# Layer 0's opening: tile 0's rows and two modulation blocks load first, and four gate tiles run as two halves over the input features

## The chip, the cores and the metric

The kernel runs on one core of a Trainium2 chip. The metric is the device time of one execution in microseconds (us). The core has five engines that work beside each other: TensorE (PE, matrix products, with its weight loads shown apart as PEld), VectorE (DVE), ScalarE (ACT), GpSimd (POOL) and SyncE (SP, which here issues most DMA transfers). Each engine takes its instructions in a fixed order. "Granted clock" is the share of full speed that TensorE ran at.

## The reference, cut to what matters

A backbone of two layers: layer 0 is windowed attention with a gate, layer 1 a bidirectional scan mixer. The change touches only the start of layer 0:

```python
shift, scale, gate = adaln(c, w_ada[i], b_ada[i])         # silu(c) @ w_ada + b_ada, split in 3
shift_c, scale_c, gate_c = adaln(c_ctx, w_ada[i], b_ada[i])
u  = rms_normalize(h)  * (1.0 + scale[:, None]) + shift[:, None]
uc = rms_normalize(hc) * (1.0 + scale_c) + shift_c
...
q, k, v, g = jnp.split(h @ w_in, [...], axis=-1)          # h is u or uc here
...
y_lat = ((o * jax.nn.silu(g)) @ w_out)
```

There are 1024 latent rows, 256 context rows and 1024 features, all in float32.

## The kernel before, in words

Everything is held transposed: features on the 128 partitions (8 tiles `k` of 128 features), rows along the free axis. The rows form three tiles `i`: tile 0 and tile 1 with 512 latent rows each, tile 2 with the 256 context rows. A float32 matrix product is done as three products of rounded halves: `mm3` (L225 to L231) multiplies the high half of the weights `wh` with the high and the low half of the rows (`uH`, `uL`), and the low half `wl` with `uH`. `load_w` loads a weight tile into a `wr` buffer (7 of them); ACT rounds it to `wh` (L215) and POOL subtracts to get `wl` (L217), four buffers each. `load_halves` does a weight tile as two halves over the input features.

The opening is `norm0`. It needs shift and scale: four blocks `n` of the modulation weights (0 and 1 are shift, 2 and 3 scale; 0 and 2 serve features k = 0 to 3, 1 and 3 serve k = 4 to 7). `ada0` multiplies one block with the condition on TensorE (L372), copies the row on ACT and turns it into a column (`modulation`). The blocks use eight `wada` buffers, four for each block. For each tile of rows, `stats` squares on ACT, adds the eight squares (L416, on POOL), and `rstd_c` sums over partitions on TensorE (L354), takes root and reciprocal and spreads the factor r with another product (L361, copied by ACT in L363). `modulate` then makes `uH` and `uL` of each k. It has two forms: without POOL, DVE multiplies by scale and r (L296), ACT adds the shift and rounds (L297), DVE adds and subtracts (L298); with POOL, POOL multiplies by r (L291), DVE scales and shifts (L292), ACT rounds (L293), DVE subtracts (L294). `N0P` says for how many k of each tile the form with POOL is used.

After it, `qkvg` runs on tile 0 the four gate tiles (`g_step`, `g_out`), then for each tile the two k tiles (`kproj`, with the rotation `rope` on DVE and POOL) and the v blocks of 128 rows (`vproj`, weights `wv`, copied from `pj` by ACT in L541 and DVE in L542). `pj` has four banks. `v` and the k tensors lie in a pool that takes the memory of norm0's pool, so they can be written only once what lay there has been used. Later come the q tiles, other gates and the modulation columns of the rest, and attention.

The order on each engine is made when the program is built: a scheduler takes, among the instructions that are ready by its own estimate of time, the one with the lowest place in the program. `high_priority(offset=-U0OFF[i])` shifts the places of a block: `U0OFF` of 100 puts it 100 places later, -200 puts it 200 places earlier. `issue_after(ins)` keeps the transfers that a block issues behind `ins` on its queue. The order of the loads is modulation block 0, tile 0's rows, blocks 2, 1 and 3 (`XORD`), the weights of the first two gates, tile 1's rows, the rope tables, tile 2's rows, the other weights.

Of the kernel before, what the change touches and what calls it, by code (L numbers as in the profile page):

```python
# [9 lines left out]
F32 = mybir.dt.float32  # L10
# [3 lines left out]
ALU = mybir.AluOpType  # L14
# [3 lines left out]
P = 128  # L18
D = 1024
KT = D // P  # L20
LAT = 1024
# [4 lines left out]
TT = [(0, 512), (512, 512), (1024, 256)]  # L26

HEADS = 16
KV = 4
HD = 64  # L30
# [12 lines left out]
    pj=1, S=2, pt=2, pv=1,  # L43
# [1 line left out]
    oraw=3, h1=2, h1k=8, wada=8, sqa=1,  # L45
    cacc=2, cctx=1, bT=2, cT=2, xn4=4, xn2=1, bn4=4, bn2=1, sz=2, xw=2, hf=2, hx=2, M=2, y2=1, xs=1, uT=2, pj2=2, psX=3, sk=2, dg=2,
)
N0P = (0, 4, 4)
ADAO = 0
XORD = (0, "x", 2, 1, 3)  # L50
VLAST = 0
G0 = 4
U0OFF = (0, 100, 200)
AHEAD = 1
PACE = 4
PARTS = 8
# [51 lines left out]
class Kernel:  # L108
# [196 lines left out]
    def layer0(self):  # L305
        nc, t, a = self.nc, self.t, self.a
        cps = ExitStack()
        BUFS.update(S=1, pj=4, wr=7, qf=2, ql=2, wh=4, wl=4)
        self.psA = self.pool("psA", space=PSUM, ctx=cps)
        NB = (LAT + CTX) // P  # L310
        self.uH, self.uL = [None] * 3, [None] * 3
        cw = ExitStack()
        wvp = self.pool("wv", ctx=cw)

        self.cs = t(wvp, [P, KT, 32], F32, "cs32")
        nc.vector.memset(self.cs, 0.0)
        nc.vector.tensor_copy(self.cs[:, :, 0:2], self.csf)
        self.wp = self.pool("wq", ctx=cw)
        p = self.pq = self.pool("qp", ctx=cw)
        c0 = ExitStack()  # L320
        n0 = self.norm0(c0)
        next(n0)
        wg = [self.load_halves(a["wg"][x], nc.gpsimd) for x in range(2)]
        next(n0)
        self.load_rope(p, 0, LAT)
        next(n0)
        c0.close()
        ckv = ExitStack()
        kvp = self.pool("kv", ctx=ckv, side="right")
        self.v = t(kvp, [P, NB, KV, 2 * HD], F32R, "v")  # L330
        self.kHH = [t(kvp, [P, LAT + CTX], F32R, f"kHH{j}") for j in range(KV)]
        self.kL = [t(kvp, [P, LAT + CTX], F32R, f"kL{x}") for x in range(KV // 2)]
        self.mask = t(kvp, [P, 1152], BF16, "mask")
        self.nsink = t(kvp, [P, HEADS], F32, "nsink")
        self.sink = t(kvp, [P, HEADS], F32, "sink")
        self.qkvg(p, wg, wvp)
        if "u" in self.dump:
            for i, (s, n) in enumerate(TT):
                self.dump_split("u", self.uH[i], self.uL[i], i, n, s)
        cw.close()  # L340
        cps.close()
        with ExitStack() as c1:
            BUFS.update(S=2, pj=1)
            self.psA = self.pool("psT", space=PSUM, ctx=c1)
            self.attention(c1, ckv)
            BUFS.update(pj=2)

    def rstd_c(self, pool, acc, n, width, size=512, rout=None, dout=None):

        nc, t, ps = self.nc, self.t, self.psA  # L350
        nb = n // P
        pn = t(ps, [P, 512], F32, self.ptag)
        for b in range(nb):
            nc.tensor.matmul(pn[:, b : b + 1], acc[:, b * P : (b + 1) * P], self.ones[:, 0:1], start=True, stop=True)  # L354
# [6 lines left out]
        nc.tensor.matmul(pr[:, :n], self.ones, dg.rearrange("p b n -> p (b n)"), start=True, stop=True)  # L361
        r = t(*(rout or (pool, [P, size], F32, f"rr{size}")))[:, :n]
        nc.scalar.copy(r, pr[:, :n])  # L363
        return r
# [9 lines left out]
        nc.scalar.copy(row, pj)  # L374
        self.modulation(0, n, row, ps)

    def norm0(self, c0):

        nc, t = self.nc, self.t
        ps = self.psA  # L380
        p1 = self.p0 = self.pool("n0", ctx=c0, side="right")

        u = self.up
        hin, hs = {}, {}
        raws = {}

        def load_x(i):
            src = self.xin(i).rearrange("(k p) n -> p k n", p=P)
            if i == 0:
                x = t(u, [P, KT, 512], F32, "uL1")  # L390
                hin[i] = [x[:, :4], x[:, 4:]]
            elif i == 1:
                hin[i] = [t(u, [P, KT // 2, 512], F32, tag) for tag in ("uH2", "uL2")]
            else:
                hin[i] = [t(p1, [P, 2, 512], F32, "wada").rearrange("p k n -> p (k n)").rearrange("p (k n) -> p k n", k=4) for _ in range(2)]
            hs[i] = [x[:, k] for x in hin[i] for k in range(4)]
            for e in range(2):
                ld = nc.sync.dma_start(hin[i][e], src[:, 4 * e : 4 * e + 4])
            return ld

        def load_ada(n):
            raws[n] = [t(p1, [P, 2, 512], F32, "wada") for e in range(4)]
            for e in range(4):
                ld = nc.sync.dma_start(raws[n][e], self.a["w_ada"][0, n, 2 * e : 2 * e + 2].rearrange("k p c -> p k c"))
            return ld

        def stats(i):
            n = TT[i][1]
            acc = t(p1, [P, 512], F32, "sqa")[:, :n]
            for k in range(KT):  # L410
                if k == 0:
                    nc.scalar.activation(acc, hs[i][k], AF.Square)
                else:
                    sq = t(p1, [P, 512], F32, "sqt")[:, :n]
                    nc.scalar.activation(sq, hs[i][k], AF.Square)
                    nc.gpsimd.tensor_tensor(acc, acc, sq, op=ALU.add)  # L416
            return self.rstd_c(p1, acc, n, D)

        for n in XORD:
            if n == "x":  # L420
                load_x(0)
            else:
                ld = load_ada(n)
        with self.tc.issue_after(ld.ins):
            yield
            ld = load_x(1)
        with self.tc.issue_after(ld.ins):
            yield
            load_x(2)
        r = stats(0)  # L430
        if ADAO:
            for n in (0, 2, 1, 3):
                self.ada0(n, raws[n], ps)
            for k in range(8):
                self.alloc_u(0) if k == 0 else None
                self.modulate(0, hs[0][k], r, 0, k, N0P[0] > k)
        else:
            for e in range(2):
                for n in (e, 2 + e):
                    self.ada0(n, raws[n], ps)  # L440
                if e == 0:
                    self.alloc_u(0)
                for k in range(4 * e, 4 * e + 4):
                    self.modulate(0, hs[0][k], r, 0, k, N0P[0] > k)
# [6 lines left out]
        yield  # L451

    def rope(self, pool, ps, i, out):
        nc = self.nc
# [49 lines left out]
    def g_step(self, p, w, x, i):  # L504
        self.g_out(p, self.proj_h(self.psA, w, self.uH, self.uL, i), x, i)

    def qkvg(self, p, wg, wvp):
# [8 lines left out]
        self.q_d = [[t(self.dr, [4, 2, HD, n], F32, f"q{j}_{i}") for i, (_, n) in enumerate(TT)] for j in range(KV)]  # L516
        self.sg_d = [[t(self.dr, [2, P, n], F32, f"sg{j}_{i}") for i, (_, n) in enumerate(TT)] for j in range(KV)]


        for x in range(G0):  # L520
            self.g_step(p, wg[x] if x < 2 else self.load_halves(a["wg"][x], nc.gpsimd), x, 0)
        wk = [self.load_halves(a["wk"][x], nc.gpsimd) for x in range(2)]
        wv = [self.load_w(a["wv"][q // 2, :, q % 2 * 512 : q % 2 * 512 + 512], 2, 256, pool=wvp, eng=nc.gpsimd) for q in range(4)]

        def kproj(x, i):
# [35 lines left out]
        n = [3, 3, 3, 2]  # L561
# [983 lines left out]
```

## Time and profile before

| | |
|---|---|
| time, median of 3 runs | 1880.89 us (1879.43 to 1883.35) |
| the profiled execution's own time | 1880.79 us, span 1878.7 us |
| mean granted clock of TensorE | 0.98 |
| busy shares of the span | PE 95%, DVE 63%, ACT 48%, POOL 40% |
| the opening, 0 to 104 us | first gate matmul at 35.19, first k matmul of tile 1 at 104.16 |

A row of the timeline gives the start, the length, the engine, the line, the operation, the output and input by the program's names, the shape and the count, and in brackets how long the engine had stood idle and what ended that. A row with a count above one spans from the first start to the last end. A row of a group gives busy time and mean length of one in ns; a row of waits gives who waited for whom, the sum, the number of times and the longest.

### The profile page before, as it was taken

How to read it: one execution, taken by the hardware profiler on the slowest of the kernel's cores; microseconds unless marked ns; L12 is line 12 of the kernel's file. 1: busy time of each engine (PE TensorE's matmuls, PEld its weight loads, DVE VectorE, ACT ScalarE, POOL GpSimd, SP SyncE). 2: the span in 40 equal slices, each digit the busy share in tenths (PEclk: the TensorE clock that was granted, in tenths of full speed). 3: DMA queues.
4: the chain of work that ended last, by engine and by line, in shares of the span. 5: the costliest groups of instructions: out<-in, count | busy, mean ns of one | idle time of the engine just before them, and what ended most of it. 6: DMA issues, size and time to landing. Idle time of an engine off the chain costs nothing. (4 is left out here: it accounts for less than half of the span.)

```text
span 1878.7 us, 29635 instructions
## 1 busy us (share of the span) xinstructions
PE 1790.6 (95%) x10632; PEld 1541.9 (82%) x10632; DVE 1178.2 (63%) x2199; ACT 906.5 (48%) x1861; POOL 758.8 (40%) x1029
## 2 busy tenths in 40 slices
PE   6899998899999899979999999999999999999997
PEld 2687776788888786668898898989889898988887
DVE  3754426887777766584665758666575766754843
ACT  4522326677778665562353535434353544543632
POOL 4741107654456454302343343524335252442411
PEclk8899999999999999989999999999999999999998
DMA  9348756553345446111111111111111111433552
GB/s 357 108 118 260 240 167 157 126 126 95 97 120 134 113 129 222 59 56 34 38 36 44 47 33 44 39 41 36 44 47 33 47 38 39 141 117 100 177 153 78
DMA packets 147203, 192.10 MB, mean 102 GB/s; under 512 B 15312, under 2 KB 84816, under 8 KB 147056
## 3 DMA queue, kind: packets, MB, share of 16 engines
q1 hardware_dynamic: 112992, 171.56, 29.0%
q0 software_dynamic: 34064, 18.65, 5.5%
q8 instruction: 84, 1.38, 0.3%
q14 instruction: 63, 0.52, 0.1%
HBM read 154.54 MB, written 35.92 MB: 101 GB/s over the span
## 5 line engine op out<-in xcount | busy, mean ns | idle before, releaser
L229 PE MATMUL pj<-uH,wh 128*128 128x512 f32 (+1 forms) x712 | 259.3, 365 | 12.1 <-DVE v L542 2.8
L230 PE MATMUL pj<-uL,wh 128*128 128x512 f32 (+1 forms) x712 | 245.1, 345 | 1.3 <-DVE uL L298 0.9
L231 PE MATMUL pj<-uH,wl 128*128 128x512 f32 (+1 forms) x712 | 244.5, 344 | 1.1 <-POOL wl L217 1.1
L1059 POOL TENSOR_TENSOR xw<-xn,dtdec 128x256 f32<-128x256 f32 x144 | 105.9, 738 | 206.6 <-PE psD L1082 102.1
L984 PE MATMUL pj<-uH,wh 128*128 128x512 f32 x512 | 171.7, 405 | 1.1 <-ACT xn L951 1.1
L984 PE MATMUL pj<-uH,wl 128*128 128x512 f32 x512 | 171.8, 405 | 0.0
L229 PEld LDWEIGHTS pj<-uH,wh 128*128 128x128 f32 x712 | 136.7, 192 | 40.5 <-issue 11.9
L984 PE MATMUL pj<-uL,wh 128*128 128x512 f32 x512 | 168.3, 399 | 0.0
L217 POOL TENSOR_TENSOR wl<-wr,wh 128x512 fp32r<-128x512 f32 x96 | 127.2, 1329 | 77.7 <-ACT wh L215 67.1
L631 DVE TENSOR_TENSOR pl<-pt,ph 128x512 fp32r<-128x512 f32 x168 | 114.5, 687 | 64.6 <-ACT ph L630 63.5
L1009 PE MATMUL pj<-wh,uH 128*128 128x256 f32 x512 | 154.7, 302 | 0.0
L1009 PE MATMUL pj<-wh,uL 128*128 128x256 f32 x512 | 151.3, 295 | 0.0
L231 PEld LDWEIGHTS pj<-uH,wl 128*128 128x128 f32 x712 | 136.4, 192 | 17.7 <-POOL wl L217 1.5
L1009 PE MATMUL pj<-wl,uH 128*128 128x256 f32 x512 | 150.8, 295 | 0.0
L230 PEld LDWEIGHTS pj<-uL,wh 128*128 128x128 f32 x712 | 136.9, 192 | 14.0 <-DVE uL L298 1.4
L215 ACT CAST wh<-wr 128x512 fp32r<-128x512 f32 (+1 forms) x136 | 87.3, 643 | 116.8 <-PE pj L230 75.2
L1188 ACT ACTIVATE uT<-psX,nw 128x128 f32<-128x128 f32 x128 | 47.0, 367 | 189.9 <-PE psX L1187 188.8
L605 DVE CUSTOM_DVE_ANT_0 sm<-S,mask,nsink 128x640 f32<-128x640 f32 (+2 forms) x160 | 119.1, 772 | 26.7 <-PE S L602 13.8
L630 ACT CAST ph<-pt 128x512 fp32r<-128x512 f32 x168 | 97.6, 586 | 61.8 <-PE pt L626 56.2
L607 ACT ACTIVATE sm<-sm,nm 128x640 f32<-128x640 f32 (+2 forms) x160 | 118.5, 742 | 9.5 <-DVE nm L605 9.0
L1154 POOL TENSOR_TENSOR xs<-xn,sk 128x256 f32<-128x256 f32 x64 | 42.0, 657 | 184.8 <-DVE sk L1150 183.6
L984 PEld LDWEIGHTS pj<-uL,wh 128*128 128x128 f32 x512 | 95.6, 188 | 19.9
(330 smaller groups left out, 4990.5 us busy)
## 6 DMA issues: line engine op xcount, KB each, us to landing
wr<-w_x SPq DMA_DIRECT2D x32, 512.0 KB
wr<-wo SPq DMA_DIRECT2D x48, 256.0 KB
wr<-w_sk SPq DMA_DIRECT2D x24, 512.0 KB
wr<-wg SPq DMA_DIRECT2D x40, 256.0 KB
qs<-q POOLq DMA_DIRECT2D x40, 256.0 KB, 4.0
wada<-w_ada SPq DMA_DIRECT2D x16, 512.0 KB
wr<-wq SPq DMA_DIRECT2D x32, 256.0 KB
wl<-w_ada SPq DMA_DIRECT2D x32, 256.0 KB
```

The costliest lines, as they stand in the source:

```text
L215: nc.scalar.copy(h, raw)
L217: (eng or nc.vector).tensor_tensor(l, raw, h, op=ALU.subtract)
L229: self.nc.tensor.matmul(ps, lh, rh, start=first and i == 0, stop=False)
L230: self.nc.tensor.matmul(ps, lh, rl, start=False, stop=False)
L231: self.nc.tensor.matmul(ps, ll, rh, start=False, stop=last and i == n - 1)
L605: nc.vector.tensor_tensor_reduce(out=sm[:, :W], in0=Sv, in1=self.mask[:, m0 : m0 + W], scale=-SCALE, scalar=self.nsink[:, 4 * j + r : 4 * ...
L607: nc.scalar.activation(sm[:, :W], sm[:, :W], AF.Exp, bias=nm[:, r : r + 1], scale=-1.0, accum_out=sums[:, r : r + 1])
L630: nc.scalar.copy(ph, ptf)
L631: nc.vector.tensor_sub(pl, ptf, ph)
L984: nc.tensor.matmul(raw[:, 512 * i : 512 * i + 512], l[:, k, :], r[i][:, k, :], start=k + y == 0, stop=k == KT - 1 and y == 2)
L1009: nc.tensor.matmul(pj[:, c], l, r[:, k, :], start=c % 2 + q + k + y == 0, stop=c % 2 == 1 and q == 1 and k == 3 and y == 2)
L1059: nc.gpsimd.tensor_tensor(xw, X(st, c).rearrange("p (r h) -> p r h", r=R), self.dtdec[:, c, hd(d, g)].unsqueeze(2).broadcast_to([P, R, HP] ...
```

## The change

- `norm0` loads tile 0's rows, then modulation blocks 0 and 2, then the first input halves (512 of 1024 features) of the four gate weights, then blocks 1 and 3, the second gate halves, the weights of k, tile 1's rows, the rope tables, tile 2's rows.
- Tile 0's squares are added on DVE, not on POOL. Its rows are multiplied by r in place for all eight k (eight more DVE operations); then for each half of the features two modulation blocks are worked out, four k are scaled, shifted, rounded and subtracted, and the four gate tiles get their matmuls of that half, each into a `pj` bank of its own that is held over both halves. `g_out` follows after the second.
- Tile 2 uses the form with POOL for all eight k (`N0P` 8 where it was 4), and the blocks of tile 1 and tile 2 have places 200 and 100 earlier (`U0OFF`) where they were 100 and 200 later.
- `rstd_c` is cut in two functions, and the tensors `q_d` and `sg_d` are declared earlier; neither adds an instruction.

```diff
-N0P = (0, 4, 4)
-ADAO = 0
-XORD = (0, "x", 2, 1, 3)
+N0P = (0, 4, 8)
-U0OFF = (0, 100, 200)
+U0OFF = (0, -200, -100)
...
-                    nc.gpsimd.tensor_tensor(acc, acc, sq, op=ALU.add)
+                    (nc.vector if i in (0,) else nc.gpsimd).tensor_tensor(acc, acc, sq, op=ALU.add)
...
-        for n in XORD:
...
+        def gates(e):
+            return [self.load_w(a["wg"][x][:, e * 512 : (e + 1) * 512], 4, eng=nc.gpsimd) for x in range(G0)]
+        last = lambda: self.tc.issue_after(ld.ins)
+        load_x(0)
+        load_ada(0)
+        ld = load_ada(2)
+        with last():
+            wg = gates(0)
         r = stats(0)
...
+        for k in range(KT):
+            nc.vector.tensor_mul(hs[0][k], hs[0][k], r)
+        self.alloc_u(0)
+        m = self.mod[0]
+        for e in range(2):
+            for n in (e, 2 + e):
+                self.ada0(n, raws[n], ps)
+            for k in range(4 * e, 4 * e + 4):
+                h, uh = hs[0][k], self.uH[0][:, k, :]
+                nc.vector.tensor_scalar(out=h, in0=h, scalar1=m[:, 8 + k, 0:1], scalar2=m[:, k, 0:1], op0=ALU.mult, op1=ALU.add)
+                nc.scalar.copy(uh, h)
+                nc.vector.tensor_sub(self.uL[0][:, k, :], h, uh)
+            if e == 0:
+                pj = [t(ps, [P, 512], F32, "pj") for _ in range(G0)]
+            for x in range(G0):
+                self.mm3(pj[x], [(wg[x][0][:, k], wg[x][1][:, k], self.uH[0][:, 4 * e + k, :], self.uL[0][:, 4 * e + k, :]) for k in range(4)], e == 0, e == 1)
+                if e == 1:
+                    self.g_out(p, pj[x], x, 0)
+            if e == 0:
+                load_ada(1)
+                ld = load_ada(3)
+                with last():
+                    wg = gates(1)
+                    wk = [self.load_halves(a["wk"][x], nc.gpsimd) for x in range(2)]
+                    ld = load_x(1)
+                with last():
+                    self.load_rope(p, 0, LAT)
+                    load_x(2)
         for i in (1, 2):
             with self.tc.high_priority(offset=-U0OFF[i]):
...
-        for x in range(G0):
-            self.g_step(p, wg[x] if x < 2 else self.load_halves(a["wg"][x], nc.gpsimd), x, 0)
-        wk = [self.load_halves(a["wk"][x], nc.gpsimd) for x in range(2)]
```

More of the change, by code (lines that the diff above doesn't have):

```diff
@@ L320, in layer0 @@
         c0 = ExitStack()
[L321 to L326, printed above, removed]
+        self.q_d = [[t(self.dr, [4, 2, HD, n], F32, f"q{j}_{i}") for i, (_, n) in enumerate(TT)] for j in range(KV)]
+        self.sg_d = [[t(self.dr, [2, P, n], F32, f"sg{j}_{i}") for i, (_, n) in enumerate(TT)] for j in range(KV)]
+        wk = self.norm0(c0, p)
         c0.close()
@@ L335, in layer0 @@
         self.sink = t(kvp, [P, HEADS], F32, "sink")
-        self.qkvg(p, wg, wvp)
+        self.qkvg(p, wk, wvp)
         if "u" in self.dump:
@@ L350, in rstd_c, with rstd_n @@
         nc, t, ps = self.nc, self.t, self.psA
+        pn = t(ps, [P, 512], F32, self.ptag)
+        for b in range(n // P):
+            nc.tensor.matmul(pn[:, b : b + 1], acc[:, b * P : (b + 1) * P], self.ones[:, 0:1], start=True, stop=True)
+        return self.rstd_n(pool, pn, n, width, size, rout, dout)
+    def rstd_n(self, pool, pn, n, width, size=512, rout=None, dout=None):
+        nc, t, ps = self.nc, self.t, self.psA
         nb = n // P
-        pn = t(ps, [P, 512], F32, self.ptag)
-        for b in range(nb):
-            nc.tensor.matmul(pn[:, b : b + 1], acc[:, b * P : (b + 1) * P], self.ones[:, 0:1], start=True, stop=True)
         rc = t(pool, [P, 4], F32, "rc", 2)[:, :nb]
@@ L375, in ada0, with norm0 @@
         self.modulation(0, n, row, ps)
-    def norm0(self, c0):
-        nc, t = self.nc, self.t
+    def norm0(self, c0, p):
+        nc, t, a = self.nc, self.t, self.a
         ps = self.psA
@@ L415, in stats @@
                     nc.scalar.activation(sq, hs[i][k], AF.Square)
-                    nc.gpsimd.tensor_tensor(acc, acc, sq, op=ALU.add)
+                    (nc.vector if i in (0,) else nc.gpsimd).tensor_tensor(acc, acc, sq, op=ALU.add)
             return self.rstd_c(p1, acc, n, D)
-        for n in XORD:
[L420 to L426, printed above, removed]
@@ L427, in norm0 @@
-        with self.tc.issue_after(ld.ins):
-            yield
-            load_x(2)
-        r = stats(0)
-        if ADAO:
-            for n in (0, 2, 1, 3):
-                self.ada0(n, raws[n], ps)
[L434 to L444, printed above, removed]
+        def gates(e):
+            return [self.load_w(a["wg"][x][:, e * 512 : (e + 1) * 512], 4, eng=nc.gpsimd) for x in range(G0)]
@@ L450, in norm0 @@
                     self.modulate(0, hs[i][k], r, i, k, N0P[i] > k)
-        yield
+        return wk
     def rope(self, pool, ps, i, out):
@@ L505, in g_step, with qkvg @@
         self.g_out(p, self.proj_h(self.psA, w, self.uH, self.uL, i), x, i)
-    def qkvg(self, p, wg, wvp):
+    def qkvg(self, p, wk, wvp):
         nc, t, a = self.nc, self.t, self.a
@@ L515, in qkvg @@
         kh_d = [[t(self.dr, [P, n], F32, f"k{x}_{i}") for i, (_, n) in enumerate(TT)] for x in range(2)]
-        self.q_d = [[t(self.dr, [4, 2, HD, n], F32, f"q{j}_{i}") for i, (_, n) in enumerate(TT)] for j in range(KV)]
-        self.sg_d = [[t(self.dr, [2, P, n], F32, f"sg{j}_{i}") for i, (_, n) in enumerate(TT)] for j in range(KV)]
-        for x in range(G0):
-            self.g_step(p, wg[x] if x < 2 else self.load_halves(a["wg"][x], nc.gpsimd), x, 0)
-        wk = [self.load_halves(a["wk"][x], nc.gpsimd) for x in range(2)]
         wv = [self.load_w(a["wv"][q // 2, :, q % 2 * 512 : q % 2 * 512 + 512], 2, 256, pool=wvp, eng=nc.gpsimd) for q in range(4)]
```

## The prediction

> **What bounds the kernel now.** I read the page first, then the stretches, the waits of TensorE in the opening, and the timeline of one engine at a time.
>
> ```profile
> PE 1790.6 (95%) x10632; PEld 1541.9 (82%) x10632; DVE 1178.2 (63%) x2199; ACT 906.5 (48%) x1861; POOL 758.8 (40%) x1029
> ```
>
> TensorE is busy 95% of the span, so an edit that leaves its work alone can only pay where TensorE stands still or runs slowly. The change touches the first 104 us, so I cut those into stretches (columns: stretch and length, busy time and count of PE, PEld, DVE, ACT, POOL, then granted clock, DMA share, GB/s).
>
> ```profile
> 20.00:35.00 15.00, 12.85 (x76) 5.47 (x70) 4.94 (x9) 5.21 (x9) 5.01 (x5) 0.93 1.05 385
> 35.00:54.00 19.00, 13.76 (x46) 10.67 (x47) 15.52 (x13) 12.18 (x23) 18.43 (x12) 0.70 0.82 295
> 54.00:82.00 28.00, 28.00 (x119) 22.68 (x119) 17.79 (x17) 15.23 (x28) 25.90 (x21) 0.96 0.46 144
> 82.00:88.00 6.00, 6.00 (x53) 6.00 (x52) 6.00 (x11) 2.37 (x4) 1.51 (x1) 1.00 0.00 0
> 88.00:104.00 16.00, 8.40 (x53) 7.84 (x51) 15.88 (x32) 7.24 (x17) 9.88 (x14) 0.79 0.41 89
> ```
>
> Up to 35 us the DMA engines are full (385 GB/s). From 35 to 54 POOL is full (18.43 of 19 us) and TensorE gets 46 matmuls done. From 54 to 88 TensorE is full. From 88 to 104 DVE is full (15.88 of 16) and TensorE busy for half. The two waits of TensorE there:
>
> ```profile
> PE pt L361 <- ACT qh L478: 4.9, 1, 4.9
> PE pj L229 <- DVE v L542: 2.8, 1, 2.8
> ```
>
> The second is the one that counts. After it TensorE starts the k projection of tile 1:
>
> ```profile
> 104.16 0.77 PE L229 MATMUL pj<-uH,wh 128*128 128x512 f32 x1 [2.83 <-DVE v L542]
> ```
>
> It waited for a free bank of `pj`. All four held v blocks of tile 0, whose copies could not be written:
>
> ```profile
> 102.96 1.20 ACT L541 CAST v<-pj 128x256 fp32r<-128x256 f32 x4 [0.60 <-DVE uL L294]
> ```
>
> The copies waited for the last modulation of tile 2 (L294): `v` lies where norm0's pool was, and that is free only then. So the opening ends with a chain on POOL and DVE: square sums of tile 1, its modulation, the modulation of tile 2, the v copies. I take 104.16 us as the mark and ask when the changed kernel reaches it. Behind it TensorE is nearly full, so a shift there should reach the end.
>
> The chain's rows, first on POOL:
>
> ```profile
> 13.87 9.37 POOL L416 TENSOR_TENSOR sqa<-sqa,sqt 128x512 f32<-128x512 f32 x7 [12.48 <-ACT sqt L415]
> 33.07 6.64 POOL L217 TENSOR_TENSOR wl<-wr,wh 128x512 fp32r<-128x512 f32 x4 [9.83 <-DMA wr<-wg]
> 39.67 10.86 POOL L416 TENSOR_TENSOR sqa<-sqa,sqt 128x512 f32<-128x512 f32 x7
> ```
>
> then what starts and ends them on ACT, PE and DVE:
>
> ```profile
> 12.64 0.63 ACT L412 ACTIVATE sqa<-uL 128x512 f32<-128x512 f32 x1 [0.99 <-DMA uL<-xT]
> ```
> ```profile
> 28.44 0.59 ACT L363 COPY rr<-pt 128x512 f32<-128x512 f32 x1 [3.80 <-PE pt L361]
> ```
> ```profile
> 35.19 0.80 PE L229 MATMUL pj<-uH,wh 128*128 128x512 f32 x2 [0.61 <-ACT uH L297]
> ```
> ```profile
> 38.16 0.63 ACT L412 ACTIVATE sqa<-uH 128x512 f32<-128x512 f32 x1 [0.67 <-DMA uH<-xT]
> ```
> ```profile
> 70.12 1.02 PE L361 MATMUL pt<-sqt,ones 128*128 128x512 f32 x2
> ```
> ```profile
> 71.95 6.53 DVE L296 SCALAR_TENSOR_TENSOR uL<-uL,mod,rr 128x512 f32<-128x512 f32 x4
> ...
> 90.28 0.67 DVE L294 TENSOR_TENSOR uL<-uH,uH 128x512 fp32r<-128x512 f32 x1
> ...
> 95.05 3.60 DVE L296 SCALAR_TENSOR_TENSOR wada<-wada,mod,rr 128x256 f32<-128x256 f32 x4
> ...
> 101.85 1.08 DVE L294 TENSOR_TENSOR uL<-wada,uH 128x256 fp32r<-128x256 f32 x3
> ```
>
> Tile 1's square sums are ready at 39.67 + 10.86 = 50.5, yet its factor r leaves TensorE (L361) only at 70.1: the old offset of 100 places puts it behind the gates. Then DVE needs 71.95 to 90.95 for tile 1 and 95.05 to 102.93 for tile 2.
>
> **The change, part by part.** *Opening loads.* Ahead of the first gate matmul lie 6.3 MB (rows of tile 0 and modulation blocks 0 and 2, 2.1 MB each) instead of 10.5 MB (all four blocks). One half of a tile's rows is 1.05 MB, and 1.05 MB / 385 GB/s is 2.72 us. Tile 0's first half was complete at 3.1 MB and in use at 12.64; the change has both halves at 2.1 MB, so near 9.9, and block 2, which ends at 6.3 MB, at 12.64 + 3 x 2.72 = 20.8. The seven sums of tile 0 move from POOL (9.37 us) to an idle DVE at about 0.7 each, the size of the 0.67 us row above: four are left after 9.9, done near 13. From the end of the sums to r took 13.87 + 9.37 = 23.2 to 29.0, 5.8 us, so r is there at 19, and eight added multiplications on DVE (8 x 0.7) end at 24.5. The first gate matmul followed the arrival of the last block (10.5 MB, 12.64 + 7 x 2.72 = 31.7) by 3.5 us; here both inputs give about 24.5, plus an add-multiply and a cast, some 25.5, against 35.19. That is 9.7 us earlier, and by itself worth nothing: TensorE would meet the same chain.
>
> *The gates in halves.* As many matmuls as before; four `pj` banks are held from the first half to the end of the second, and nothing else asks for a bank then. Gates and tile 0's k are 144 matmuls, at 28.00 / 119 = 0.235 us 33.9 us; v of tile 0 is 96 at 6.00 / 53 = 0.113, 10.9 us. From 25.5 without a wait that ends at 70. If all 96 gate matmuls ran at double the interval (the stretch from 35 had a clock of 0.70) it is 93. Warm TensorE has 18 us of slack to what follows.
>
> *Tile 1's rows move back.* 14.7 MB now lie up to and with their first half (rows 2.1, modulation 8.4, two gate halves 2.1, wk 1.05, itself 1.05), against 12.6: 38.16 + 2 x 2.72 = 43.6. The rope tables and tile 2's rows follow; nobody asks for them before. On SP these loads stand behind wk's, whose buffers come free with POOL's splits of the gates; I cost that at nothing, since the DMA engines are full until then; were they not, each us by which SP issues the rows late is one at the mark. Blocks 1 and 3 wait on SP for the eight buffers of 0 and 2, as two of the four blocks do now, with the second gate halves, wk and tile 1's rows queued behind them.
>
> *Priorities.* Tile 1's block moves from 100 places late to 200 early, tile 2's from 200 late to 100 early. Sums begin 1.5 us after the rows (39.67 - 38.16) and take 9.4 to 10.9 us: 45.1 to 56.0 by the dearer. Then r by the 5.8 of tile 0: 61.8. The wait for the gates on TensorE, up to 10 us, is gone. Tile 1 on DVE: the 19.0 us it took, with tile 0's rope between: 80.8. Tile 2: r no longer late, and with all eight multiplications on POOL DVE does 16 short operations (mean ns behind the comma):
>
> ```profile
> L298 DVE SCALAR_TENSOR_TENSOR uL<-wada,mod,uH 128x256 fp32r<-128x256 f32 x4 | 1.8, 470 | 0.0
> L292 DVE TENSOR_SCALAR wada<-wada,mod 128x256 f32<-128x256 f32 x4 | 1.7, 417 | 0.0
> L294 DVE TENSOR_TENSOR uL<-wada,uH 128x256 fp32r<-128x256 f32 x4 | 1.5, 406 | 0.0
> ```
>
> 8 x (0.417 + 0.406) = 6.6 us instead of 7.9: 87.4. The copies to the mark took 104.16 - 102.93 = 1.2: 88.6. Cheapest, with no rope between (4.6 us less) and sums in 9.4: 82.5. Dearest, with tile 2's r late by as much as now (4.1): 92.7.
>
> *POOL as a check.* These are its means in the first 104 us:
>
> ```profile
> L217 POOL TENSOR_TENSOR wl<-wr,wh 128x512 fp32r<-128x512 f32 x16 | 23.2, 1469 | 10.5 <-DMA wr<-wg 9.8 <-ACT wh L215 0.7
> L416 POOL TENSOR_TENSOR sqa<-sqa,sqt 128x512 f32<-128x512 f32 x14 | 19.3, 1377 | 13.4 <-ACT sqt L415 12.5
> L291 POOL TENSOR_TENSOR uH<-uH,rr 128x512 f32<-128x512 f32 x4 | 6.6, 1678 | 0.0
> L416 POOL TENSOR_TENSOR sqa<-sqa,sqt 128x256 f32<-128x256 f32 x7 | 6.5, 925 | 0.6 <-ACT sqt L415 0.5
> ```
> ```profile
> L291 POOL TENSOR_TENSOR wada<-wada,rr x4: 747/917/929, 95.0 to 97.4; 128x256 f32<-128x256 f32 x4
> ```
>
> From 45.1: sums 10.9, wk and wv 8 x 1.469 = 11.8, tile 1's four 6.6, tile 2's sums 6.5, its eight 8 x 0.9 = 7.2: 43.0, ending at 88.1. POOL therefore has no room left, and ends with the DVE chain. I put the mark at 89: 15.2 us early. Sum: 1880.8 - 15.2 = **1865.6 us**, on the profiled execution's own 1880.79 (span 1878.7 and 2.1 around it), which is 0.1 from the median, 1880.89.
>
> **The rivals.** *DVE and POOL take turns.* DVE's first-stage operation of tile 1 and POOL's beside it stretch each other (min/median/max ns):
>
> ```profile
> L296 DVE SCALAR_TENSOR_TENSOR uL<-uL,mod,rr x12: 745/1760/1828, 31.4 to 76.7; 128x512 f32<-128x512 f32 x12
> L291 POOL TENSOR_TENSOR uH<-uH,rr x4: 1480/1742/1747, 74.5 to 79.6; 128x512 f32<-128x512 f32 x4
> ```
> ```profile
> 60.98 0.73 POOL L416 TENSOR_TENSOR sqa<-sqa,sqt 128x256 f32<-128x256 f32 x1
> 61.91 1.29 POOL L217 TENSOR_TENSOR wl<-wr,wh 128x512 fp32r<-128x512 f32 x1 [0.20 <-ACT wh L215]
> ```
>
> If they never overlapped, undisturbed times add: POOL from 45.1, 19 long ones at 1.29 and 15 short at 0.73, 35.5; DVE, tile 1 about 10.5, tile 2 6.6, rope 3: the mark falls at 45.1 + 55.6 + 1.2 = 101.9, a gain of 2.3, 1878.5. For it: a DVE operation of 0.745 takes 1.76. Against it: a pair takes about 1.65 (four in 6.6 us), less than 0.745 + 1.29 = 2.04. The Trainium skill's page "SBUF — State Buffer", section "Who interferes with whom", states this as an exclusive lock: a DVE instruction with two SBUF inputs and a GpSimd one that reads SBUF exclude each other for the whole instruction. By that rule the time would be this rival's; the trace agrees in kind and not in full size.
>
> *Weights behind the normalisation: slower.* The new places put tiles 1 and 2 ahead of the splits of wk and wv on POOL. If POOL does all of both tiles first, it ends at 45.1 + 10.9 + 6.6 + 6.5 + 7.2 = 76.3, plus a wait for tile 2's r of 5.8: 82.1. Two halves of wk 2.9 (85.0), k of tile 0 48 x 0.235 = 11.3, v 10.9, and about 1.7 of slow clock after the stop: the mark at 108.9, 4.7 late: 1885.5. It decides once wk's splits start after about 77. For it: POOL has no slack. Against: wk's data is there before tile 1's rows, and POOL waits 5.8 us for r(1), room for four splits.
>
> *TensorE stops in line.* Its queue is fixed; if tile 1's column sums stand amid the second gate half and sums end at 56, half the gates (48 x 0.235) and k and v follow: 56 + 2 + 33.5 + slow clock 1.7 = 93, with a second such stop of 4.9 as now 98: gain 6, 1875. *The chain runs undisturbed*: mark at 80 to 82.5, 1857 to 1859.
>
> *It does nothing*: were the mark set by tile 1's arrival, 5.4 us later now, the gain would be lost; but r waits 20 us behind arrival and sums today, so this I count with the first rival.
>
> **How the numbers follow.** Forecast case (mark 86 to 92) 0.48; undisturbed 0.14; TensorE stops 0.19; taking turns 0.08; slower 0.11. About 0.2% (3.8 us) is what a measurement here can tell from no change. Faster by more: 0.48 + 0.14, of the stops 0.17 and of the turns 0.03, together 0.82; within: 0.02 of the stops and 0.05 of the turns, 0.07; slower: 0.11. The range 1855 to 1878 leaves out the slower case, part of the turns, and a few per cent at the fast end.
>
> **What would show it.** First gate matmul near 25.5; L361 of tile 1 near 61 instead of 70; tile 2's last L294 near 87; the first k matmul of tile 1 near 89; after it the same durations. Wrong if wk's splits start after 77 or L361 waits 5 us in the gates.

## The result, and the profile after

| | before | after |
|---|---|---|
| time, median of 7 runs each | 1880.89 us (1878.67 to 1885.53) | 1889.6 us (1886.3 to 1895.12) |
| ratio, 95% interval | | 1.0048 [1.0031, 1.0065] |
| the profiled execution: own time, span | 1880.79, 1878.7 us | 1888.01, 1886.0 us |
| the mark, first k matmul of tile 1 | 104.16 us | 111.24 us |
| from the mark to the end of the span | 1774.5 us | 1774.8 us |

The change made the kernel slower by 0.5%; the forecast was 0.8% faster. The mark came 7.1 us later and the span grew by 7.3: the whole difference lies ahead of the mark. Line numbers are those of the changed file (L227 to L229 were L229 to L231, L548 and L549 were L541 and L542). The mark and the copy of `v` ahead of it:

```profile
109.54 1.18 ACT L548 CAST v<-pj 128x256 fp32r<-128x256 f32 x4
111.24 0.77 PE L227 MATMUL pj<-uH,wh 128*128 128x512 f32 x1 [9.54 <-DVE v L549]
```

TensorE now stands 9.54 us at the place where it stood 2.83. The same stretches as before (busy time and count of PE, PEld, DVE, ACT, POOL, granted clock, DMA share, GB/s):

```profile
20.00:35.00 15.00, 11.93 (x56) 5.97 (x53) 13.17 (x19) 5.35 (x10) 5.66 (x4) 0.89 1.05 385
35.00:54.00 19.00, 14.35 (x78) 9.67 (x76) 5.71 (x8) 8.42 (x15) 11.53 (x9) 0.89 0.94 341
54.00:82.00 28.00, 27.41 (x120) 22.59 (x121) 16.53 (x16) 17.56 (x31) 22.30 (x17) 0.89 0.35 114
82.00:88.00 6.00, 4.22 (x34) 3.82 (x32) 6.00 (x10) 1.62 (x4) 3.00 (x3) 1.00 0.00 0
88.00:104.00 16.00, 9.36 (x53) 8.93 (x53) 12.31 (x18) 5.45 (x10) 8.63 (x10) 0.79 0.09 33
104.00:112.00 8.00, 0.76 (x2) 0.69 (x3) 7.86 (x20) 3.52 (x10) 7.44 (x13) 0.53 0.59 98
```

From 20 to 35 us DVE gets 13.17 us of work done instead of 4.94: tile 0 does start early. From 35 to 54 it does 5.71 instead of 15.52, and that is more than was won. Why it stops is seen on TensorE and DVE:

```profile
28.60 1.45 PE L227 MATMUL pj<-uH,wh 128*128 128x512 f32 x4 [2.33 <-ACT uH L440]
29.98 1.92 PE L372 MATMUL aps<-wada,cs 128*32 128x512 f32 x4
42.45 2.78 PE L372 MATMUL aps<-wada,cs 128*32 128x512 f32 x24
45.16 1.05 PE L201 MATMUL pt<-sel,arow 128*128 128x2 f32 x8
46.26 0.17 DVE L203 TENSOR_TENSOR mod<-pt,bada 128x8 f32<-128x8 f32 x1 [12.66 <-PE pt L201]
51.35 2.07 PE L227 MATMUL pj<-uH,wh 128*128 128x512 f32 x4 [3.00 <-ACT uH L440]
```

The first gate matmul is at 28.60. A few products of block 1 (L372) run at 29.98, so its data had begun to land; the other 24 products of blocks 1 and 3 stand in TensorE's queue behind the first halves of all four gates and run at 42.45. DVE waits 12.66 us for their column, and the second halves start at 51.35. Behind them comes tile 1, first its factor on ACT:

```profile
62.91 0.62 ACT L213 CAST wh<-wr 128x512 fp32r<-128x512 f32 x1 [5.66 <-PE pj L228]
63.54 1.28 ACT L510 ACT_TABLE_LOAD   x1
64.84 0.60 ACT L510 ACTIVATE qf<-pj 128x512 f32<-128x512 f32 x1
65.45 1.28 ACT L356 ACT_TABLE_LOAD   x1
66.75 0.26 ACT L356 ACTIVATE rc<-pt,eps 128x4 f32<-128x4 f32 x1
72.28 0.60 ACT L363 COPY rr<-pt 128x512 f32<-128x512 f32 x1
```

The root (66.75) stands in ACT's queue behind a weight cast that waits 5.66 us for a buffer which the second gate halves still read, behind a tanh of a gate, and behind two table loads. Tile 1's last sum on POOL was done at 54.80 + 3.16 = 57.96, but TensorE's sum over the partitions (L348, L354 in the file before) comes only at 63.39, in line behind matmuls of the second gate halves, without an idle time before it:

```profile
45.29 2.62 POOL L417 TENSOR_TENSOR sqa<-sqa,sqt 128x512 f32<-128x512 f32 x2 [2.74 <-ACT sqt L416]
54.80 3.16 POOL L417 TENSOR_TENSOR sqa<-sqa,sqt 128x512 f32<-128x512 f32 x2 [1.61 <-ACT sqt L416]
63.39 0.95 PE L348 MATMUL pt<-ones,sqa 128*128 128x1 f32 x8
```

Then tile 1 and tile 2 on DVE (first and last operation of each), with what stands between them:

```profile
72.91 6.21 DVE L294 SCALAR_TENSOR_TENSOR uL<-uL,mod,rr 128x512 f32<-128x512 f32 x4 [0.31 <-ACT rr L363]
92.78 2.36 DVE L292 TENSOR_TENSOR uL<-uH,uH 128x512 fp32r<-128x512 f32 x2
96.38 0.62 ACT L491 CAST qh<-qf 128x512 fp32r<-128x512 f32 x1 [4.10 <-DVE qf L474]
98.31 0.26 ACT L356 ACTIVATE rc<-pt,eps 128x2 f32<-128x2 f32 x1
101.31 1.53 DVE L290 TENSOR_SCALAR wada<-wada,mod 128x256 f32<-128x256 f32 x2 [2.08 <-POOL wada L289]
109.11 0.98 DVE L292 TENSOR_TENSOR uL<-wada,uH 128x256 fp32r<-128x256 f32 x2
```

Tile 1 takes 72.91 to 95.14, tile 2 101.31 to 110.09. Between them lie 6.2 us in which r of tile 2 is made: its root is at 98.31, in ACT's queue behind a cast of tile 0's k (L491) that waits 4.10 us for DVE.

### The profile page after: what moved, and what is told of

Same layout as the page of the kernel before. It is cut to its first block, busy times and chain, and to the rows that moved or that the text cites. A ratio compares the mean times of both kernels' runs of the same rounds, so it can differ in the third digit from the quotient of the medians.

```text
span 1886.0 us, 29647 instructions
## 1 busy us (share of the span) xinstructions
PE 1790.8 (95%) x10632; PEld 1543.2 (82%) x10632; DVE 1186.5 (63%) x2214; ACT 906.5 (48%) x1863; POOL 751.1 (40%) x1026
## 5 line engine op out<-in xcount | busy, mean ns | idle before, releaser
L227 PE MATMUL pj<-uH,wh 128*128 128x512 f32 (+1 forms) x712 | 258.8, 365 | 27.1 <-DVE v L549 9.5
L229 PE MATMUL pj<-uH,wl 128*128 128x512 f32 (+1 forms) x712 | 245.0, 344 | 1.3 <-POOL wl L215 1.3
L227 PEld LDWEIGHTS pj<-uH,wh 128*128 128x128 f32 x712 | 136.9, 193 | 55.8 <-issue 19.1
L229 PEld LDWEIGHTS pj<-uH,wl 128*128 128x128 f32 x712 | 136.3, 192 | 17.7 <-POOL wl L215 1.7
L612 DVE CUSTOM_DVE_ANT_0 sm<-S,mask,nsink 128x640 f32<-128x640 f32 (+2 forms) x160 | 119.2, 772 | 23.2 <-PE S L609 11.9
```

The source lines that it names most:

```text
L227: self.nc.tensor.matmul(ps, lh, rh, start=first and i == 0, stop=False)
L229: self.nc.tensor.matmul(ps, ll, rh, start=False, stop=last and i == n - 1)
L612: nc.vector.tensor_tensor_reduce(out=sm[:, :W], in0=Sv, in1=self.mask[:, m0 : m0 + W], scale=-SCALE, scalar=self.nsink[:, 4 * j + r : 4 * ...
```

## The experiments

Ratios are to the kernel before, in runs of the same chip; the medians of different experiments come from different chips. "Mark" is the first k matmul of tile 1 in the profiled execution, r(1) and r(2) are the factors r of tile 1 and tile 2, and "copied at" is the start of the copy in L363.

One trace is one execution. The first gate matmul is at 28.60 in the change, and at 26.74 to 29.48 in four runs whose edits lie behind it (the old form, tile 2 out, `v` moved, part of `v` out of the way). From the mark to the end the traces of the experiments take 1773.4 to 1784.6 us. So 2 or 3 us between the times of two traces decide nothing, and the mark gives the time only to some us.

**Places and form undone.** Two runs put one constant back each.

```diff
-U0OFF = (0, -200, -100)
+U0OFF = (0, 100, 200)
```

> The changed kernel with only the old places of the blocks of tile 1 and tile 2 (U0OFF 100 and 200 later). Theory A (the products of modulation blocks 1 and 3 stand behind the first gate halves on TensorE, so tile 0's second half is modulated only at 49 to 58 us, and ACT then holds tile 1's root behind work that waits for the second gate halves): the places are not the cause, this stays at 1886 to 1893 us, tile 1's factor r is copied at 72 us or later. Theory B (the early places of tiles 1 and 2 push tile 0's and the weights' work back): the loss goes, 1881 us or less.

Measured: 1889.66 us, 1.0038 [1.0023, 1.0054], mark 114.69, r(1) copied at 87.30: as theory A had it.

```diff
-N0P = (0, 4, 8)
+N0P = (0, 4, 4)
```

> The changed kernel with only N0P back to 4 for tile 2. Theory C (eight multiplications on POOL that can start only with tile 2's r pace its modulation): the modulation of tile 2 takes about 8 us instead of 8.8 and the whole is 1 us or less faster, 1888.5. Theories A and B: no change beyond that, 1888 to 1890 us.

Measured: 1887.95 us, 1.003 [1.0016, 1.0044], mark 106.12. Neither alone gives the loss back; the two intervals overlap with the change's own. That points to the loads, the sums and the gates in halves. It doesn't show it, since no run puts both constants back at once; the run with all products ahead of the gates, below, keeps both.

**Places and form alone.** The counterpart: the kernel before with both constants.

```diff
-N0P = (0, 4, 4)
+N0P = (0, 4, 8)
-U0OFF = (0, 100, 200)
+U0OFF = (0, -200, -100)
```

> The kernel before with two constants of the change alone: the blocks of tiles 1 and 2 have their places 200 and 100 earlier, and tile 2 takes the form with POOL for all eight k. Loads, sums and gates stay as before. Theory M (the time is the mark, the first k matmul of tile 1, plus about 1776; the mark is set by the chain sums of tile 1, its factor r, tile 1 on DVE, tile 2, v copies): with the old loads the sums end at 50.5 as before; with the root placed early r(1) is copied near 60 instead of 71.2, tile 1 ends near 82, tile 2 near 92, mark 93 to 98: 1869 to 1875, faster by 6 to 12. Theory W (weights behind the normalisation: the early places put the splits of wk behind tile 1 on POOL, and TensorE lacks weights): the mark is at 104 to 110, 1881 to 1886. Theory P (the places do little, as their undoing in the change did little): 1879 to 1884.

Measured: 1887.15 us, 1.0032 [1.0019, 1.0045], mark 108.65. r(1) is copied at 64.16 instead of 71.20, so the earlier root is real, and yet the kernel is slower. From 54 us on TensorE has these waits of over 1 us, which the kernel before has not (line numbers of the file before):

```profile
PE pj L229 <- DVE qf L498: 5.7, 2, 4.0
PE pj L231 <- POOL wl L217: 2.8, 1, 2.8
```

Tile 1's early modulation is ahead of other work on the same engines: the gates' last step (L498, which frees a `pj` bank) on DVE, and a split of wk on POOL. From 54 to 82 us TensorE gets 77 matmuls done instead of 119:

```profile
54.00:82.00 28.00, 21.34 (x77) 16.26 (x75) 22.15 (x20) 14.80 (x28) 26.39 (x20) 0.87 0.27 88
```

This is the prediction's rival of the weights behind the normalisation, with the banks as a second strand, in a kernel that has only the constants. In the change itself no such wait is seen.

**Is the mark tied to tile 2?** The change without tile 2's statistics and modulation; its rows are only rounded and subtracted, so its part of the output is left unnormalised.

```diff
+                if i == 2:
+                    self.alloc_u(i)
+                    for k in range(KT):
+                        nc.scalar.copy(self.uH[i][:, k, :], hs[i][k])
+                        nc.vector.tensor_sub(self.uL[i][:, k, :], hs[i][k], self.uH[i][:, k, :])
+                    continue
```

> The change with tile 2's statistics and modulation left out: its rows are only rounded and subtracted (its rows come out unnormalised). Theory M: the mark follows tile 1's end instead of tile 2's, 95 to 98 and a v copy, so 97 to 102 instead of 111.2, with no wait of 9.5 us on TensorE: 1876 to 1882, 8 to 14 faster than the change, though no matmul of the projections is taken out. Theory T (the change lost its time on TensorE itself, by the stretch of half clock and the gates in two halves, and the wait of 9.5 us at the mark is only where it shows): the wait is replaced by later matmuls, 1886 to 1890.

Measured: 1880.24 us, 0.9988 [0.9978, 0.9997].

```profile
99.70 0.50 PE L227 MATMUL pj<-uH,wh 128*128 128x512 f32 x1 [2.40 <-DVE v L555]
```

The mark falls from 111.24 to 99.70 and the time by 9.4 us (11.3 by the ratios), though no projection is taken out and r(1) is copied no earlier (74.84). So the time hangs on tile 2's end.

**v moved, first attempt.** The change with two k tensors placed ahead of `v` in their pool.

> The changed kernel with v given a place in its pool that does not lie over tile 2's rows (two kHH tensors are placed before it); no instruction is added or taken away. Theory M (the start of tile 1's k products waits for four pj banks, these for the v copies, these for the end of tile 2's modulation because of the memory): the wait of 9.5 us before tile 1's first k matmul goes, and the time falls by 6 to 10 us, 1880 to 1884. If the v copies wait for something else: unchanged, 1889 us.

Measured: 1892.42 us, 1.0059 [1.0035, 1.0083], mark 113.70, wait on the v copies 9.53. It decides nothing: by the addresses of the built program the last 320 bytes (of each partition) of one of tile 2's two buffers still lay under `v`, and the order on ACT was unchanged, with the v copies behind tile 2's casts.

**Products earlier.** The change with the products of blocks 1 and 3 placed 100 earlier.

```diff
+            with self.tc.high_priority(offset=100 * e):
+                for n in (e, 2 + e):
+                    self.ada0(n, raws[n], ps)
```

> The changed kernel with the products and columns of modulation blocks 1 and 3 given a place 100 earlier, so that they stand between the matmuls of the first gate halves. Theory A: block 3's column is ready near 38 us instead of 49, tile 0's second half 8 to 10 us earlier, tile 1's r is copied near 64 us instead of 72, the first k matmul of tile 1 comes at 101 to 104 instead of 111, and the time is 1878 to 1883 us. Theory B: TensorE does the second gate halves earlier but tile 1's r and the end do not move, 1887 to 1890 us.

Measured: 1895.32 us, 1.0068 [1.0048, 1.0088], mark 116.00. The scheduler dealt the products out among the gate matmuls in groups of four:

```profile
36.30 1.05 PE L372 MATMUL aps<-wada,cs 128*32 128x512 f32 x4
37.28 0.50 PE L228 MATMUL pj<-uL,wh 128*128 128x512 f32 x1
```

From the start of a group to the next gate matmul are 0.98 us here; 24 in one piece took 2.78 in the change, 0.46 for four. The last column came at 50.77 instead of 47.30. The edit made them later, so the theory was not tried by it.

**The root ahead on ACT.** wk's weights (loads, casts) and the tanh of the gates issued behind the root of tile 1, whose rows load ahead of wk and whose sums stand in the program ahead of the second gate halves.

> The change with one order altered: on ACT the casts of wk and the tanh of the gates stand behind the root of tile 1, and tile 1's sums are traced before the second gate halves. Theory Q (r(1) lost its time in the in-order queues: the root stood behind a cast and a tanh that wait for the second gate halves): r(1) is copied at 62 to 66 instead of 72.3, tile 1 ends near 88, the mark at 102 to 106: 1880 to 1885. Theory D (DVE and POOL take turns, so an earlier r only stretches tile 1): r(1) earlier by some us, but tile 1 takes 26 us or more and the mark stays within 2 us of 111: 1888 to 1891.

Measured: 1889.07 us, 1.0049 [1.0032, 1.0066], mark 110.60. r(1) is copied at 59.65, 12.6 us earlier than in the change, and the time is the same.

```profile
54.24 1.86 PE L348 MATMUL pt<-ones,sqa 128*128 128x1 f32 x8 [10.53 <-POOL sqa L417]
54.00:82.00 28.00, 15.68 (x53) 12.35 (x54) 19.28 (x28) 12.90 (x27) 17.10 (x16) 0.56 0.13 38
```

The column sums of tile 1 (L348) came to stand ahead of the columns of blocks 1 and 3, TensorE waited 10.5 us there, DVE had nothing at all from 35 to 54, and afterwards TensorE ran at a granted clock of 0.56. The second gate halves start at 72.72 instead of 51.35, and the mark has no wait: TensorE itself is late. The time lies in theory D's range, but not by its mechanism, since tile 1 took 18.4 us (64.78 to 83.14) and not 26. ACT's queue delays r(1); what that costs alone this run can't say, as it changed TensorE's order too.

**Root and products.** As before this, with the products of blocks 1 and 3 in one piece behind two gates.

> As the one before, and on TensorE the products of modulation blocks 1 and 3 stand in one piece behind the first halves of two gates instead of all four. Theory Q: the columns of blocks 1 and 3 are there near 41 instead of 47, tile 0's second half ends 4 to 6 us earlier, r(1) is copied at 60 to 64, the mark at 100 to 104: 1878 to 1882. If the interleaving of products and gate matmuls costs as much in one piece as it did in groups of four: no gain over the run before it, 1880 to 1886. Theory D: 1887 to 1891.

Measured: 1890.42 us, 1.0047 [1.0032, 1.0062], mark 112.29. A miss for the theories with an earlier column, and no test of theory D, whose range it lies in. The 32 products were done sooner, but their columns (L201) stood in TensorE's queue behind the other two gates, and r(1) came at 72.95:

```profile
39.88 3.64 PE L378 MATMUL aps<-wada,cs 128*32 128x512 f32 x32
49.03 0.95 PE L201 MATMUL pt<-sel,arow 128*128 128x2 f32 x8
```

**All products ahead of the gates.** The four modulation blocks load and are multiplied first, as before the change; the gates stay in halves that follow each other.

```diff
-        load_ada(0)
-        ld = load_ada(2)
+        for n in (0, 2, 1, 3):
+            ld = load_ada(n)
...
+        for e in range(2):
+            with self.tc.issue_after(mm.ins):       # mm: the last product
+              for x in range(G0):
+                self.mm3(...)
```

> The change with all four modulation blocks loaded ahead of the gate weights and all four products ahead of the first gate matmul on TensorE, as before the change; the gates stay in two halves, which now follow each other. Theory H (the early first halves cost the time: the products of blocks 1 and 3 stand behind them, DVE idles for 12.7 us, and the second halves, the tanh and the root of tile 1 behind it on ACT come late): first gate matmul 33 to 35, the columns of blocks 1 and 3 near 36 instead of 47, gates done near 59 instead of 69, r(1) copied at 63 to 66, tile 1 to 87, tile 2 to 101, mark 101 to 104: 1879 to 1882, level with the kernel before. Theory L (the gates in halves and their later weights are not what costs, the early places and the form of tile 2 are): 1886 to 1890.

Measured: 1884.48 us, 1.0008 [0.9997, 1.0018]: it can't be told from the kernel before, so the loss is gone or nearly, though both constants are the change's. The mark is where theory H had it, the time 2.5 us above its range.

```profile
33.03 0.50 PE L227 MATMUL pj<-uH,wh 128*128 128x512 f32 x1 [0.28 <-ACT wh L213]
33.60 0.97 PE L201 MATMUL pt<-sel,arow 128*128 128x2 f32 x8
62.70 4.19 DVE L359 TENSOR_TENSOR sqt<-ident,rc 128x512 f32<-128x512 f32 x1
102.78 0.76 PE L227 MATMUL pj<-uH,wh 128*128 128x512 f32 x1 [11.18 <-DVE v L549]
```

The first gate matmul is 4.4 us later than in the change, the last column 13.7 us earlier (33.60 instead of 47.30), and the mark 8.5 us earlier. Of these, r(1) brings about 3.2 us, tile 1 on DVE 2.7 (69.74 to 89.26) and the gap before tile 2 2.6 (to 92.85). r(1) is at 69.12 instead of the expected 63 to 66; 3.5 us of that are L359, 4.19 us instead of 0.69. Two things were altered together here, the order of the loads and the place of the products in TensorE's queue; no run parts them.

**Tile 2's sums early.** In addition tile 2's rows load ahead of the rope tables, its sums run on DVE ahead of tile 1's normalisation, and its r has its own buffer.

> As the one before, and tile 2's rows load ahead of the rope tables, its sums stand ahead of tile 1's normalisation and on DVE, and its factor r has a buffer of its own. Theory H with the chain read from the change's trace (a gap of 6.2 us between tile 1 and tile 2 in which r(2) is made): the gap goes, tile 2 follows tile 1 at 87, ends near 95, mark 95 to 98 or where TensorE is done with tile 0 if that is later: 1872 to 1877, faster than both kernels. If POOL, freed from the sums, instead stretches tile 1 on DVE (the two taking turns), tile 1 ends near 92 and the mark near 101: 1879.

Measured: 1882.56 us, 1.0 [0.9991, 1.001], mark 102.34, wait 11.26. A miss: tile 2's root was done at 78.24, but reciprocal and spread stood in DVE's queue behind most of tile 1, so that r(2) was copied at 90.97, as late as in the run before (91.64).

**Part of v out of the way.** Three of the ten blocks of `v` in memory of their own, taken ahead of norm0's pool, so that nothing of tile 2 lies under them. First in the kernel before, then in the last run's kernel, at last in the change itself.

```diff
+        vp = self.pool("v", ctx=ckv, side="right")
+        self.v = [t(vp, [P, KV, 2 * HD], F32R, f"v{b}") for b in range(3)]
...
-        self.v = t(kvp, [P, NB, KV, 2 * HD], F32R, "v")
+        self.v += [t(kvp, [P, KV, 2 * HD], F32R, f"v{b}") for b in range(3, NB)]
```

> The kernel before with one thing altered: three of the ten blocks of v lie in memory of their own, taken ahead of norm0's pool, so that their copies out of the pj banks need not wait for tile 2's modulation. Theory M (in both kernels the first k matmul of tile 1 waits for the v copies, which wait for tile 2's end only by the place of v in memory): the bank comes free at tile 1's end, 91 plus a copy; TensorE still stops for tile 2's r near 93 and has two v blocks to do behind it, so mark 97 to 101 instead of 104.2 and 1874 to 1878. Theory S (the bank is free early, but k of tile 1 meets the next late thing at once, rope on DVE behind tile 2): mark earlier, time 1879 to 1882.

Measured: 1880.39 us, 0.9991 [0.9982, 1.0001], mark 100.71. The mark moved as theory M expected, but the time is theory S's and can't be told from no change. The wait at the mark, 2.83 us, is gone, but TensorE still stops 5.3 us for r(2) (4.9 before; L363 is L361 of the other files) and has two blocks of v to do behind it, so there was little to win:

```profile
PE pt L363 <- ACT qh L480: 5.3, 1, 5.3
```

> The run with tile 2's sums early, and three blocks of v in memory of their own. Theory M: TensorE had ended tile 0's v at 91.1 in that run and waited 11.3 us for the copies; now it goes on at 91 to 94, mark 91 to 95: 1870 to 1875, faster than both kernels. Theory S: k of tile 1 starts early, but TensorE stops again some us later: 1877 to 1881.

Measured: 1870.66 us (1867.69 to 1871.76), 0.9935 [0.9921, 0.995]: 0.65% faster than before, and the fastest kernel of the study.

```profile
90.46 0.40 PE L227 MATMUL pj<-uH,wh 128*128 128x512 f32 x1
88.00:104.00 16.00, 15.12 (x82) 13.21 (x83) 15.36 (x29) 5.15 (x13) 8.41 (x10) 1.00 0.05 17
```

The mark is at 90.46 without a wait, 11.9 us earlier than without the edit, and the time is 11.9 lower (the two ran on different chips; by the ratios it is 0.65%, 12.2). TensorE is busy for 15.12 of the 16 us in which it had 9.36 in the change. The same edit without tile 2's sums early was not run, so what they add to it is not known.

> The change with one thing altered: three of the ten blocks of v lie in memory of their own, taken ahead of norm0's pool. Theory M (the 7 us are lost because tile 2's end, 7 us later, holds the v copies and so the first k matmul of tile 1): TensorE goes on when r(2) is spread at about 99.5 and two thirds of a v block are done, mark 100 to 103 instead of 111.2, the wait of 9.5 us gone or below 3: 1879 to 1883. Theory H alone (the first halves ahead of the products are what costs, wherever v lies): the second gate halves, r(1) and tile 1 are as late as before and k of tile 1 waits for tile 1's own end, 95 to 97, so nothing is left to wait for and the time is also near 1881; the two differ only if the mark stays above 106, 1886 to 1890, which refutes both.

Measured: 1882.4 us (1876.21 to 1890.34), 1.0006 [0.9989, 1.0023], mark 101.74 without a wait:

```profile
99.92 0.67 PE L363 MATMUL pt<-sqt,ones 128*128 128x256 f32 x2
101.74 0.40 PE L227 MATMUL pj<-uH,wh 128*128 128x512 f32 x1
```

With the wait for tile 2's memory taken away and nothing else, the change is level with the kernel before, as theory M had it. So the late chain costs its time through `v`. TensorE still passes through r(2) (L363), made as late as in the change, so the gain ends there. It is no gain over the kernel before with the same edit either (0.9991): the early start brought nothing that these runs can tell.

## Why the prediction was wrong

Right was the frame: the mark decides, and in this pair nothing changes behind it. +7.1 at the mark against +7.3 in the span, and the runs without tile 2's work and with `v` out of the way show the mark to be held by tile 2's end through the v copies. Right were also the start of tile 1's square sums (45.1 foretold, 45.29 measured), r of tile 0 (19 and 19.73 + 0.58 = 20.3), and the last term, copies to the mark (1.2 and about 1.1). The first gate matmul was 3.1 us late (25.5 and 28.60), which by itself was worth nothing, as said.

The mark was put at 89 (88.6 by the sum) and came at 111.24. The sum's own terms account for it (r is ready at the end of its copy, as in the sum):

| step | foretold | measured | missed by |
|---|---|---|---|
| r(1) ready | 61.8 | 72.88 | 11.1 |
| tile 1 on DVE | 19.0 | 22.2 | 3.2 |
| gap before tile 2 | 0 | 6.2 | 6.2 |
| tile 2 on DVE | 6.6 | 8.8 | 2.2 |

The first step that failed is in the part on the gates in halves: "From 25.5 without a wait that ends at 70". The working counted gate matmuls and forgot whose results the second halves need. The products of blocks 1 and 3 are in the same TensorE queue; the early first halves went ahead of them, and DVE stood 12.66 us for a column. All the time won at the start was lost there; the run with all products first starts its gates 4.4 us later and is 0.40% faster (1.0008 against 1.0048). Not all of the 12.66 us is the queue. Up to the end of block 3 lie 11.5 MB, and tile 0's rows (2.1 MB) were in use at 9.86; at 385 GB/s the last product's data was there near 34, an estimate, so about 8 us (to 42.45) are TensorE's order. The end of tile 0 moved too: its k matmuls end at 80.05 in the trace, and v at the 10.9 us of the sum gives 91 instead of 70, so the 18 us of slack were gone and TensorE alone would have missed 89. That TensorE's queue is fixed was said in the rival of TensorE stopping in line, but only for tile 1's column sums.

The second, and the largest miss of a term, is "Then r by the 5.8 of tile 0: 61.8. The wait for the gates on TensorE, up to 10 us, is gone". From the sums' end (57.96, foretold 56.0) to r it took 14.9 us instead of 5.8. L361 did leave the place behind the gates, but the wait for them stayed in two other places. On TensorE the column sums (L348) stood in line 5.4 us behind matmuls of the second halves, the place that the rival of TensorE stopping in line had named. On ACT, whose queue the prediction never followed, the root came 2.4 us after them, behind a cast and a tanh that wait for the second gate halves, and the copy of r 2.7 us after L361, behind two more tanhs and casts. The trace of before had shown the kind: there, too, tile 1's factor was ready for L361 only 8.6 us after its sums (50.5), mostly because DVE was busy with tile 0:

```profile
52.68 4.71 DVE L298 SCALAR_TENSOR_TENSOR uL<-uL,mod,uH 128x512 fp32r<-128x512 f32 x4
57.58 1.59 DVE L359 TENSOR_TENSOR sqt<-ident,rc 128x512 f32<-128x512 f32 x1
```

This is read from the rows; the run that removes the wait on ACT (root ahead) brings r(1) 12.6 us forward and loses it again on TensorE, so how much it costs alone stays open.

The third is "r no longer late" for tile 2. Its sums on POOL ended only at 92.2, with tile 1's multiplications and splits in between. Then the root stood 5.0 us on ACT (93.28 to 98.31) behind the cast that waits for DVE, and spread and multiplications followed. TensorE waited for the sums too:

```profile
92.27 1.01 PE L348 MATMUL pt<-ones,sqa 128*128 128x1 f32 x4 [5.78 <-POOL sqa L417]
```

The durations of DVE were mis-sized in the direction of the rival of taking turns. Tile 2's sixteen operations were priced at the means of before, 0.417 and 0.406 us, where no multiplication of POOL lay beside them; with all eight multiplications on POOL they took

```profile
L290 DVE TENSOR_SCALAR wada<-wada,mod 128x256 f32<-128x256 f32 x8 | 4.8, 604 | 2.1 <-POOL wada L289 2.1
L292 DVE TENSOR_TENSOR uL<-wada,uH 128x256 fp32r<-128x256 f32 x8 | 4.9, 613 | 0.1
```

0.604 and 0.613: 9.7 us of work instead of 6.6, overlapping a little in the rows. While POOL multiplied (to 106.61) single ones took 0.81 and 0.94, after it 0.40 and 0.41. Two steps that were foretold as dangers did not come: the splits of wk and wv were done on POOL between 57.9 and 74, not after 77, and tile 1's rows did not come late.

The range reached to 1878 and gave the slower side 0.11. The slower rival was one mechanism with one price, while five engines' queues had been reordered; the early places and the form alone are slower by 0.3%, and the change without the places by 0.4%.

## What to carry to other kernels

When work is moved forward, write down for each engine's queue what it now stands ahead of, and follow who waits for that: here an early half of a matmul held back the small products that the other half needed. Where a wait is removed from a chain, look for the next instruction on every engine of the chain, not only on the one where the trace showed the wait. And before making a chain shorter, ask why its end holds anyone at all: six kilobytes for each partition for three blocks of `v`, which cut the link between tile 2 and TensorE, gave 11.9 us with the products first and tile 2's sums early, and 0.42% in the change itself, about what the best reordering gave (0.40%). In the kernel before they gave nothing that can be told (0.9991): TensorE stopped there for r(2) all the same.

## What the runs showed of the hardware

Two things were not expected. A DVE operation beside back-to-back work on POOL can take several times as long: L359 (two inputs in the state buffer, 0.69 us in the change) took 4.19 us in the run with all products first, while POOL did seven splits without a pause:

```profile
56.95 8.71 POOL L215 TENSOR_TENSOR wl<-wr,wh 128x512 fp32r<-128x512 f32 x7
```

The extra 3.5 us are 2.8 splits of 1.24, so DVE stood for more than one of POOL's operations. With tile 2's sums early the same operation took 3.09, again beside seven splits. The Trainium skill, "SBUF — State Buffer", section "Who interferes with whom", says that a DVE instruction with two inputs there contends with a GpSimd instruction that reads there, and that the shared port is an exclusive lock. The rows agree with a full stop of DVE (in the second run it ends at 67.26, 0.55 us after POOL's burst), and show in addition that POOL can go first more than once in a row.

The second is the cost of dealing 32-column products out among 128-column matmuls: 0.98 us for a group of four against 0.46 in one piece, both at a granted clock of 1.00.
